# First layer of a four-layer decoder trunk: another order of loads, splits and transposes

## The chip, the core and the metric

The kernel runs on one core of a Trainium2 chip. The metric is the device time of one execution in microseconds (us), the median of several runs of the same program.

## The reference

Four residual layers follow each other, each `x = x + mixer(rms_norm(x, gain))`, on one sequence of 256 tokens with 1024 channels, all in float32. The mixers are of the kinds A, B, C, A. Only the beginning of the first one matters here:

```python
def rms_norm(x, g):
    y = x * lax.rsqrt(jnp.mean(x * x, axis=-1, keepdims=True) + EPS)
    return y * g

def mixer_a(h, w_in, v_gain, w_s, b_s, w_out):
    proj = h @ w_in                                   # (256, 1024) @ (1024, 6144)
    u = proj[..., :2048]
    v = rms_norm(proj[..., 2048:4096], v_gain)
    z = proj[..., 4096:]
    mixed = ...                                       # per chunk and group: tril(w_s) @ v + b_s
    return (u * mixed * jax.nn.silu(z)) @ w_out
```

## The kernel before

**Three products for one.** Every float32 operand is cut into a high part (a value of TensorE's fast float32 type, made by ACT) and a low part (what is left, made by DVE). A product of two such operands is three matmuls: high by high, high by low, low by high. In the list of engines PE is TensorE, ACT is ScalarE, DVE is VectorE, POOL is GpSimd, SP is SyncE.

**The weight stream.** All weights come through one stream of units `wr` of 128 x 1024 values (two K tiles of 128 rows by 512 columns). SP issues the loads (`load_units`, line 135) into four raw buffers, ACT writes the high part (`w0h`, `w1h`, ..., line 82), DVE the low part (`w0l`, ..., line 85), and a raw buffer comes free, so that SP loads the unit four further on, when DVE has written the low part. Seven pairs of split units are kept.

**The first projection (`proj_first`).** It makes the first 512 columns of `v` for both token tiles t = 0, 1 (two PSUM banks, `v_0` and `v_1`). K has eight tiles k = 0 to 7, in four pairs u. `turn(u)` is four TensorE transposes that bring the pair u of x, both token tiles, into one PSUM bank `hp`; `high(k)` is ACT's high part of h for one k, both token tiles (128x256, line 330, from `hp` to `hT`, with the gain `gT` as its scale); `low(k)` is DVE's low part (line 334); `w_high` and `w_low` split half a unit; `products(k)` is the six matmuls of one k (lines 77, 78, 79 in `mm3`). The row norms of x aren't needed here: their factor is put on later, and ACT takes the sums of squares (line 225) when the projection has been issued. Each engine works off its instructions in the order in which they stand in the code.

**After it** come the second `v` projection (units 4 and 5, then 6 and 7) and so on. Between them ACT squares the first projection's banks (line 494), DVE multiplies them with the gain (line 495), and both split the result (`v00h`, `v00l`) before they split unit 6.

**The loads at the start.** SP issues, in this order: x of token tile 0, columns 0 to 511 (256 KB); the first half of unit 0 (256 KB); x of token tile 1, columns 0 to 511; the second half of unit 0; unit 1 (512 KB); the other halves of x; units 2 and 3; a gain. ACT issues the 16 KB load of `gT`. TensorE does 13 transposes of an identity matrix (line 217) before there is data.

Of the kernel before, what the change touches and what calls it, by code (L numbers as in the profile page):

```python
# [10 lines left out]
F32 = mybir.dt.float32  # L11
F32R = mybir.dt.float32r
BF16 = mybir.dt.bfloat16
# [4 lines left out]
P = 128  # L18
D = 1024
S = 256  # L20
KT = D // P
HALF = 512
DEPTH = 4
# [25 lines left out]
def hybrid_trunk_kernel(ctx, tc, x, wts, norm_gainT, a_v_gain, a_wsT, a_bsT, b_gl, b_gv, c_scaleT,  # L49
                        masks, rope, rcnt, out):  # L50
    nc = tc.nc
    n_units = wts.shape[0]

    cp = ctx.enter_context(tc.tile_pool(name="cp", bufs=1))
# [4 lines left out]
    def pp(name):  # L59
        return ps.tile([P, HALF], F32, tag="pp", name=name, bufs=4)  # L60
# [7 lines left out]
    def tiny(n, name, tag="t"):  # L68
        return cp.tile([P, n], F32, tag=f"{tag}{n}", name=name, bufs=8)

    def pair(pool, shape, tag, name, bufs):
        return (pool.tile(shape, F32R, tag=tag + "h", name=name + "h", bufs=bufs),
                pool.tile(shape, F32R, tag=tag + "l", name=name + "l", bufs=bufs))

    def mm3(out_ap, lh, rh, start, stop):

        nc.tensor.matmul(out_ap, lh[0], rh[0], start=start, stop=False, skip_group_check=True)  # L77
        nc.tensor.matmul(out_ap, lh[0], rh[1], start=False, stop=False, skip_group_check=True)  # L78
        nc.tensor.matmul(out_ap, lh[1], rh[0], start=False, stop=stop, skip_group_check=True)  # L79

    def hi_of(hi, src):
        nc.scalar.activation(hi, src, AF.Copy)

    def lo_of(lo, src, hi):
        nc.vector.tensor_tensor(lo, src, hi.bitcast(F32), op=ALU.subtract)
# [16 lines left out]
    def tick():  # L102
        now[0] += 1
        if rms_due[0] and rms_due[0][0] <= now[0]:
            rms_due[0][1]()
            rms_due[0] = None
        for e in list(tasks):
            if e[0] <= now[0]:
                try:
                    e[0] = now[0] + next(e[1])  # L110
                except StopIteration:
                    tasks.remove(e)
# [12 lines left out]
    raws = []  # L125
    units = []
# [4 lines left out]
    def load_units(n):  # L131
        while loaded[0] < min(n, n_units):
            u = loaded[0]
            raw = wp.tile([P, 2, HALF], F32, tag="wr", name=f"wr{u}", bufs=RAW_BUFS)
            nc.sync.dma_start(raw, wts[u].rearrange("p (k n) -> p k n", n=HALF))
            raws.append(raw)
            loaded[0] += 1
# [3 lines left out]
    def split_hi(n):  # L141

        while split[0] < min(n, n_units):
            u = split[0]
            load_units(u + 1)
            hi, lo = pair(wp, [P, 2, HALF], "w", f"w{u}", W_BUFS)
            hi_of(hi, raws[u])
            units.append((hi, lo))
            split[0] += 1

    def split_units(n):

        split_hi(n)
        while lowered[0] < min(n, n_units):
            u = lowered[0]
            lo_of(units[u][1], raws[u], units[u][0])
            lowered[0] += 1
            load_units(u + 1 + RAW_BUFS)
# [14 lines left out]
            split_units(used[0] + ahead)  # L173


    xt = [cp.tile([P, D], F32, tag=f"x{t}", name=f"x{t}") for t in range(2)]

    def load_x(t, n):
        nc.sync.dma_start(xt[t][:, n * HALF:(n + 1) * HALF], x[t * P:(t + 1) * P, n * HALF:(n + 1) * HALF])


    raws.append(wp.tile([P, 2, HALF], F32, tag="wr", name="wr0", bufs=RAW_BUFS))
    loaded[0] += 1
    for t in range(2):
        load_x(t, 0)
        nc.sync.dma_start(raws[0][:, t], wts[0].rearrange("p (k n) -> p k n", n=HALF)[:, t])
    load_units(2)
    for t in range(2):
        load_x(t, 1)
    load_units(RAW_BUFS)  # L190
    kc_first = cp.tile([P, 3 * D], F32, tag="kc", name="kc0")
    nc.sync.dma_start(kc_first[:, :HALF], a_v_gain[0:1, :HALF].partition_broadcast(P))
    ident = cp.tile([P, P], F32, tag="ident", name="ident")
    make_identity(nc, ident)
    m05_row = cp.tile([P, 32], F32, tag="m05", name="m05")
    m05 = m05_row[:, :4]
    nc.gpsimd.memset(m05_row[:, :8], -0.5)
    r_rows = [m05_row[:, 8 * t + 8:8 * t + 9] for t in range(2)]
    junk = cp.tile([P, HALF + 32], BF16, tag="junk", name="junk")[:, :HALF]
    hT = cp.tile([P, 2 * KT * S + 16], F32R, tag="hT", name="hT")  # L200

    def gated(layer):

# [4 lines left out]
    def h_parts(layer):  # L208

        o = 16 if gated(layer) else 0  # L210
        return [hT[:, o + i * KT * S:o + (i + 1) * KT * S].rearrange("p (k s) -> p k s", s=S) for i in range(2)]
# [3 lines left out]
    warm = atp("warm")  # L215
    for _ in range(WARM):
        nc.tensor.transpose(warm[:, :P], ident, ident)
    gT = cp.tile([P, DEPTH, KT], F32, tag="gT", name="gT")
    nc.scalar.dma_start(gT, norm_gainT)

    nc.scalar.activation(junk[:, :4], m05, AF.Square)

# [1 line left out]
    def half_ss(t, n, ss):  # L224
        nc.scalar.activation(junk, xt[t][:, n * HALF:(n + 1) * HALF], AF.Square, scale=1.0 / 32.0,  # L225
                             accum_out=ss[:, n:n + 1])

    def norm_rms(layer, t, ss):
        ms = tiny(1, f"ms{layer}{t}")
        nc.vector.scalar_tensor_tensor(ms, ss[:, 0:1], EPS, ss[:, 1:2], op0=ALU.add, op1=ALU.add)  # L230
        r = r_rows[t] if gated(layer) else tiny(1, f"r{layer}{t}")
        r_tok[t] = r
        nc.gpsimd.tensor_tensor(r, ms, m05[:, 0:1], op=ALU.pow)  # L233
        return r
# [46 lines left out]
    def h_t(k, t):  # L281
        sl = slice(t * P, (t + 1) * P)
        return hcur[0][:, k, sl], hcur[1][:, k, sl]
# [29 lines left out]
    def proj_first(name):  # L313

        o = [pp(f"{name}_{t}") for t in range(2)]
        pts = {}
        hh, hl = h_parts(0)

        def turn(u):
            pts[u] = (trp if u == 3 else atp)(f"hp0{u}").rearrange("p (k t c) -> p k t c", t=2, c=P)  # L320
            for t in range(2):
                for k in range(2):
                    nc.tensor.transpose(pts[u][:, k, t], xt[t][:, (2 * u + k) * P:(2 * u + k + 1) * P], ident)

        def part(k):
            return pts[k // 2][:, k % 2].rearrange("p t c -> p (t c)"), gT[:, 0, k:k + 1]

        def high(k):
            pt, g = part(k)
            nc.scalar.activation(hh[:, k], pt, AF.Copy, scale=g)  # L330

        def low(k):
            pt, g = part(k)
            nc.vector.scalar_tensor_tensor(hl[:, k], pt, g, hh[:, k].bitcast(F32), op0=ALU.mult, op1=ALU.subtract)

        def w_pair(u):
            units.append(pair(wp, [P, 2, HALF], "w", f"w{u}", W_BUFS))
            split[0] += 1

        def w_high(u, kk):  # L340
            hi_of(units[u][0][:, kk], raws[u][:, kk])

        def w_low(u, kk):
            lo_of(units[u][1][:, kk], raws[u][:, kk], units[u][0][:, kk])
            if kk:
                lowered[0] += 1
                load_units(u + 1 + RAW_BUFS)

        def products(k):
            w = units[k // 2]  # L350
            for t in range(2):
                mm3(o[t], h_t(k, t), (w[0][:, k % 2], w[1][:, k % 2]), k == 0, k == KT - 1)

        turn(0)
        turn(1)
        w_pair(0)
        high(0)
        w_high(0, 0)
        high(1)
        w_high(0, 1)  # L360
        w_low(0, 0)
        low(0)
        low(1)
        w_low(0, 1)
        products(0)
        products(1)
        turn(2)
        high(2)
        high(3)
        w_pair(1)  # L370
        for kk in range(2):
            w_high(1, kk)
        low(2)
        low(3)
        for kk in range(2):
            w_low(1, kk)
        products(2)
        products(3)
        turn(3)
        for u in range(2, 4):  # L380
            high(2 * u)
            high(2 * u + 1)
            split_hi(u + 1)
            low(2 * u)
            low(2 * u + 1)
            split_units(u + 1)
            products(2 * u)
            products(2 * u + 1)
        used[0] += 4
        split_units(5)  # L390
        for t in range(2):
            ss = tiny(2, f"ss_{t}")
            for n in range(2):
                half_ss(t, n, ss)
            norm_rms(0, t, ss)
        split_units(6)
        for t in range(2):
            done.add(("h", 0, t))
        for _ in range(8):
            tick()  # L400
        return o
# [75 lines left out]
    def layer_a(layer, consts, pl, mid):  # L477
        hcur[:] = h_parts(layer)
        first = proj_first(f"v{layer}0") if layer == 0 else None
        kc, wsT, bsT = consts()  # L480

# [659 lines left out]
```

## Time and profile before

| | us |
|---|---|
| median of 3 runs (lowest, highest) | 840.42 (839.43, 840.59) |
| the profiled execution, its own time | 837.59 |
| its span, first to last instruction | 835.9 |
| PE busy in the span | 828.5 (99%), 4589 matmuls |
| DVE busy | 544.0 (65%) |
| ACT busy | 491.4 (59%) |
| POOL busy | 46.6 (6%) |

The granted TensorE clock is shown as full in all of the profile's 40 slices. The DMA engines moved 149.58 MB, a mean of 179 GB/s; in the first two slices (42 us) 271 and 283 GB/s. PE has 8 tenths in the first slice, 9 or more in all others up to the last one (8).

How to read it: PE bounds the kernel as a whole, and the other engines matter where PE waits for one of them. Where PE waits, and for what, stands in the view of waits; when that was, in the timeline.

### The profile page before, as it was taken

The page shows a single profiled execution, that of the slowest core. Times are in us where ns is not written, and L with a number is a line of the kernel's source. Part 1 is how long each engine was busy: PE and PEld are TensorE (multiplying, and loading weights), DVE is VectorE, ACT ScalarE, POOL GpSimd, SP SyncE. Part 2 cuts the span into 40 slices and gives each one's busy share as a digit, 9 for nine tenths or more (in the row PEclk, how much of TensorE's full clock was granted, in tenths as well). Part 3 has the DMA queues.
Part 4 walks back from the last instruction along what each step waited for, and adds up shares of the span by engine and source line. Part 5 has one row for each costly group of instructions (what it writes and reads, how often), then busy time and mean ns, then how long its engine had stood idle before and what let it go on. Part 6 is the DMA issues. An engine that isn't in the chain of part 4 may idle for free.

```text
span 835.9 us, 12347 instructions
## 1 busy us (share of the span) xinstructions
PE 828.5 (99%) x4589; PEld 717.5 (86%) x4589; DVE 544.0 (65%) x906; ACT 491.4 (59%) x913; POOL 46.6 (6%) x71
## 2 busy tenths in 40 slices
PE   8999999999999999999999999999999999999998
PEld 6788888888988888888888889999988888888886
DVE  4786656646757677577577576898754777556551
ACT  6775444436758688687687576455544666434340
POOL 0301000000000010010010021000000000000000
PEclk9999999999999999999999999999999999999999
DMA  7876565562745355345345168447564466454541
GB/s 271 283 247 223 177 201 176 177 198 83 253 166 182 107 158 191 107 160 187 108 161 186 58 224 280 160 140 256 198 223 155 131 241 208 159 184 161 176 151 51
DMA packets 41788, 149.58 MB, mean 179 GB/s; under 512 B 4896, under 2 KB 4912, under 8 KB 41600
## 3 DMA queue, kind: packets, MB, share of 16 engines
q1 hardware_dynamic: 40608, 144.98, 52.2%
q0 software_dynamic: 976, 3.79, 1.4%
q8 instruction: 36, 0.59, 0.3%
q14 instruction: 24, 0.20, 0.1%
q10 hardware_dynamic: 144, 0.02, 0.0%
HBM read 147.72 MB, written 1.05 MB: 178 GB/s over the span
## 4 chain that ended last, share of the span: by engine, by line
PE 96%; ACT 0%; DVE 0%; issue 0%
PE wo L77 6%; PE wo L79 6%; PE wo L78 6%; PE qk L77 5%; PE qk L79 5%; PE qk L78 5%; PE v L78 5%; PE v L79 5%; PE v L77 5%; PE z L79 3%; PE z L77 3%; PE z L78 3%; PE u L78 3%; PE u L77 3%; PE u L79 3%; PE cz L77 2%
## 5 line engine op out<-in xcount | busy, mean ns | idle before, releaser
L638 POOL TENSOR_TENSOR qr<-qm,m 128x8 f32<-128x8 f32 x12 | 19.7, 1638 | 227.9 <-DVE qm L637 227.9
L633 ACT ACTIVATE junk<-qk 128x128 bf16<-128x128 f32 x96 | 26.6, 277 | 7.3 <-PE qk L79 4.7
L554 DVE SCALAR_TENSOR_TENSOR sz<-u,m,sz 128x512 f32<-128x512 f32 x16 | 11.9, 747 | 27.9 <-PE u L79 27.9
L642 ACT ACTIVATE qn<-qk,qr 128x128 f32<-128x128 f32 x96 | 27.5, 381 | 3.4 <-POOL qr L638 3.4
L447 DVE TENSOR_TENSOR x<-wo,x 128x512 f32<-128x512 f32 x16 | 11.0, 690 | 20.1 <-PE wo L79 20.0
L251 ACT ACTIVATE hT<-hp,gT 128x128 fp32r<-128x128 f32 x48 | 13.0, 383 | 14.9 <-PE hp L247 14.9
L637 DVE TENSOR_SCALAR qm<-qs 128x8 f32<-128x8 f32 x12 | 2.1, 172 | 26.7 <-ACT junk L633 26.7
L256 DVE SCALAR_TENSOR_TENSOR hT<-hp,gT,hT 128x128 fp32r<-128x128 f32 x48 | 13.5, 345 | 8.8 <-ACT hT L251 8.8
L581 ACT ACTIVATE sz<-z,m 128x512 f32<-128x512 f32 x16 | 10.7, 686 | 13.9 <-PE z L79 13.9
L633 ACT ACTIVATION_READ_ACCUMULATOR junk<-qk 128x1 f32 x96 | 18.9, 197 | 0.0
L494 ACT ACTIVATE junk<-v,m 128x512 bf16<-128x512 f32 x16 | 11.0, 685 | 11.2 <-PE v L79 11.0
L495 DVE TENSOR_TENSOR vv<-v,kc 128x512 f32<-128x512 f32 x16 | 10.7, 687 | 8.4 <-ACT junk L494 8.0
L225 ACT ACTIVATE junk<-x 128x512 bf16<-128x512 f32 x16 | 10.2, 640 | 9.6 <-DVE x L447 9.4
L557 DVE SCALAR_TENSOR_TENSOR yy<-mx,bs,sz 128x256 f32<-128x256 f32 x32 | 14.0, 480 | 0.6
L663 PE MATMUL qt<-ident,qn 128*128 128x128 f32 x96 | 14.4, 272 | 0.0
L732 ACT ACTIVATE p<-p,rl 128x384 f32<-128x384 f32 (+1 forms) x16 | 11.5, 768 | 4.8 <-DVE rl L731 4.8
L655 DVE TENSOR_TENSOR rb<-qn,kcb 128x32 f32<-128x32 f32 x96 | 13.8, 185 | 0.0
L663 PEld LDWEIGHTS qt<-ident,qn 128*128 128x128 f32 x96 | 11.7, 140 | 2.3
L233 POOL TENSOR_TENSOR r<-ms,m 128x1 f32<-128x1 f32 x4 | 3.1, 784 | 175.3 <-DVE ms L230 175.3
L728 ACT ACTIVATE p<-p,nb 128x768 f32<-128x768 f32 x8 | 7.5, 937 | 7.6 <-DVE nb L727 7.6
L651 DVE TENSOR_TENSOR ra<-qn,kcb 128x64 f32<-128x64 f32 x48 | 10.6, 221 | 1.0 <-ACT qn L642 0.4
L473 POOL TENSOR_SCALAR_AFFINE_SELECT kc<-kc 128x128 f32<-128x128 f32 x16 | 9.1, 608 | 13.9 <-DMA kc<-in_a_wsT_dram 13.9
(2779 smaller groups left out, 3264.1 us busy)
## 6 DMA issues: line engine op xcount, KB each, us to landing
wr<-in_wts_dram SPq DMA_DIRECT2D x271, 512.0 KB, 3.8
x<-in_x_dram SPq DMA_DIRECT2D x4, 256.0 KB, 4.7
kc<-in_a_wsT_dram POOLq DMA_DIRECT2D x2, 512.0 KB, 8.1
kc<-in_a_v_gain_dram POOLq DMA_DIRECT2D x1, 1024.0 KB, 4.7
out_dram<-x SPq DMA_DIRECT2D x4, 256.0 KB, 2.0
kc<-in_a_v_gain_dram POOLq DMA_DIRECT2D x1, 768.0 KB, 7.4
kcb<-in_masks_dram POOLq DMA_DIRECT2D x1, 576.0 KB, 7.3
wr<-in_wts_dram SPq DMA_DIRECT2D x2, 256.0 KB, 4.1
```

Source lines behind the costliest of these rows:

```text
L77: nc.tensor.matmul(out_ap, lh[0], rh[0], start=start, stop=False, skip_group_check=True)
L78: nc.tensor.matmul(out_ap, lh[0], rh[1], start=False, stop=False, skip_group_check=True)
L79: nc.tensor.matmul(out_ap, lh[1], rh[0], start=False, stop=stop, skip_group_check=True)
L251: nc.scalar.activation(h_parts(layer)[0][:, k, t * P:(t + 1) * P], pt[:, k % 4], AF.Copy, scale=gT[:, layer, k:k + 1])
L256: nc.vector.scalar_tensor_tensor(hTl, pt[:, k % 4], gT[:, layer, k:k + 1], hTh.bitcast(F32), op0=ALU.mult, op1=ALU.subtract)
L554: nc.vector.scalar_tensor_tensor(us[t], up[t], r_tok[t][:, 0:1], us[t], op0=ALU.mult, op1=ALU.mult)
L557: nc.vector.scalar_tensor_tensor(y[:, sl], mxs[n][t][:, sl], bsT[:, 2 * n + gg:2 * n + gg + 1], us[t][:, sl], op0=ALU.add, op1=ALU.mult)
L633: nc.scalar.activation(junk[:, :HD], ov[t][:, h], AF.Square, accum_out=ssq[t][:, h:h + 1])
L638: nc.gpsimd.tensor_tensor(rqs, ms, m05_row[:, :8], op=ALU.pow)
L642: nc.scalar.activation(qn[t][:, h], ov[t][:, h], AF.Copy, scale=rq[t][:, h:h + 1])
L655: nc.vector.tensor_tensor(rb[:, hs, s0:s0 + 16], qn[t][:, hs, s1:s1 + 16], c, op=ALU.mult)
L663: nc.tensor.transpose(pts[t][:, h], qn[t][:, h], ident)
```

## The change

The first layer's beginning is written in another order.

- x becomes one tile `xx` of 128 x 2 x 1024, with both token tiles in it. Three loads by columns take the place of four by token tile: K tiles 0 and 1 of both token tiles (256 KB, in pieces of 1 KB), K tiles 2 and 3 (256 KB), K tiles 4 to 7 (512 KB).
- ACT issues the first half of unit 0, then `gT`. SP issues x for K tiles 0 and 1, the second half of unit 0, x for K tiles 2 and 3, unit 1, the rest of x, units 2 and 3.
- `products(k)` uses the low part of the weights last: for both token tiles high by high and low (of h) by high, then for both high by low (of w).
- `turn(1)` stands behind `products(0)` instead of ahead of it; `turn(2)` behind `products(2)`; `turn(3)` behind `products(3)`.
- ACT and DVE split in that order; the high parts of units 2 and 3 come next to each other, and ahead of `high(6)` and `high(7)`.

The number of matmuls, splits and bytes stays as it is. The loads:

```diff
-    xt = [cp.tile([P, D], F32, tag=f"x{t}", name=f"x{t}") for t in range(2)]
-
-    def load_x(t, n):
-        nc.sync.dma_start(xt[t][:, n * HALF:(n + 1) * HALF], x[t * P:(t + 1) * P, n * HALF:(n + 1) * HALF])
+    xx = cp.tile([P, 2, D], F32, tag="x", name="x")
+    xt = [xx[:, t] for t in range(2)]
+
+    def load_x(k0, k1):
+
+        nc.sync.dma_start(xx[:, :, k0 * P:k1 * P], x.rearrange("(t p) c -> p t c", p=P)[:, :, k0 * P:k1 * P])
...
-    for t in range(2):
-        load_x(t, 0)
-        nc.sync.dma_start(raws[0][:, t], wts[0].rearrange("p (k n) -> p k n", n=HALF)[:, t])
+    first_unit = wts[0].rearrange("p (k n) -> p k n", n=HALF)
+    gT = cp.tile([P, DEPTH, KT], F32, tag="gT", name="gT")
+    nc.scalar.dma_start(raws[0][:, 0], first_unit[:, 0])
+    nc.scalar.dma_start(gT, norm_gainT)
+    load_x(0, 2)
+    nc.sync.dma_start(raws[0][:, 1], first_unit[:, 1])
+    load_x(2, 4)
     load_units(2)
-    for t in range(2):
-        load_x(t, 1)
+    load_x(4, 8)
     load_units(RAW_BUFS)
...
-    gT = cp.tile([P, DEPTH, KT], F32, tag="gT", name="gT")
-    nc.scalar.dma_start(gT, norm_gainT)
```

The products, and the order as it is now:

```diff
         def products(k):
-            w = units[k // 2]
-            for t in range(2):
-                mm3(o[t], h_t(k, t), (w[0][:, k % 2], w[1][:, k % 2]), k == 0, k == KT - 1)
+
+            wh, wl = (a[:, k % 2] for a in units[k // 2])
+            for t in range(2):
+                for i, h in enumerate(h_t(k, t)):
+                    nc.tensor.matmul(o[t], h, wh, start=k == 0 and i == 0, stop=False, skip_group_check=True)
+            for t in range(2):
+                nc.tensor.matmul(o[t], h_t(k, t)[0], wl, start=False, stop=k == KT - 1, skip_group_check=True)
```

```python
        turn(0)
        w_pair(0)
        high(0)
        high(1)
        low(0)
        low(1)
        for kk in range(2):
            w_high(0, kk)
            w_low(0, kk)
        products(0)
        turn(1)
        high(2)
        w_pair(1)
        w_high(1, 0)
        high(3)
        w_high(1, 1)
        low(2)
        w_low(1, 0)
        low(3)
        w_low(1, 1)
        products(1)
        products(2)
        turn(2)
        high(4)
        high(5)
        split_hi(3)
        low(4)
        low(5)
        split_units(3)
        products(3)
        turn(3)
        products(4)
        split_hi(4)
        high(6)
        high(7)
        split_units(4)
        low(6)
        low(7)
        for k in range(5, KT):
            products(k)
```

On ACT the first data instructions stand like this before (`hp_112`, `hp_117`, `hp_146`, `hp_175` are the banks of the pairs 0 to 3; L330 is `high`, L82 a high part of weights, L225 a sum of squares):

```order
L330 ACTIVATE hT<-hp_112,gT 128x256
L82 ACTIVATE w0h<-wr_66 128x512
L330 ACTIVATE hT<-hp_112,gT 128x256
L82 ACTIVATE w0h<-wr_66 128x512
L330 ACTIVATE hT<-hp_117,gT 128x256 x2
L82 ACTIVATE w1h<-wr_71 128x512 x2
L330 ACTIVATE hT<-hp_146,gT 128x256 x2
L82 ACTIVATE w2h<-wr_75 128x1024
L330 ACTIVATE hT<-hp_175,gT 128x256 x2
L82 ACTIVATE w3h<-wr_77 128x1024
L82 ACTIVATE w4h<-wr_132 128x1024
L225 ACTIVATE junk,ss_230<-x_64 128x512 x2
```

and like this now (the banks are `hp_110`, `hp_133`, `hp_162`, `hp_183`; `high` is L334, the sum of squares L229):

```order
L188 DMA wr_65<-in_wts_dram 128x512
L189 DMA gT<-in_norm_gainT_dram 128x32
...
L334 ACTIVATE hT<-hp_110,gT 128x256 x2
L82 ACTIVATE w0h<-wr_65 128x512 x2
L334 ACTIVATE hT<-hp_133,gT 128x256
L82 ACTIVATE w1h<-wr_72 128x512
L334 ACTIVATE hT<-hp_133,gT 128x256
L82 ACTIVATE w1h<-wr_72 128x512
L334 ACTIVATE hT<-hp_162,gT 128x256 x2
L82 ACTIVATE w2h<-wr_75 128x1024
L82 ACTIVATE w3h<-wr_77 128x1024
L334 ACTIVATE hT<-hp_183,gT 128x256 x2
L82 ACTIVATE w4h<-wr_125 128x1024
L229 ACTIVATE junk,ss_228<-x 128x512 x2
```

Both high parts of pair 0 now stand ahead of the first weights, and the high part of unit 3 ahead of the high parts of pair 3.

On PE the piece from the first transposes of x to the third transposes stood like this (the six matmuls of k = 0, `v_0` ahead of `v_1`; those of k = 1 follow in the same order):

```order
L323 MATMUL hp_112<-ident,x_64 128x128 x2
L323 MATMUL hp_112<-ident,x_65 128x128 x2
L323 MATMUL hp_117<-ident,x_64 128x128 x2
L323 MATMUL hp_117<-ident,x_65 128x128 x2
L77 MATMUL v_0_110<-w0h,hT 128x512
L78 MATMUL v_0_110<-w0l,hT 128x512
L79 MATMUL v_0_110<-w0h,hT 128x512
L77 MATMUL v_1_111<-w0h,hT 128x512
L78 MATMUL v_1_111<-w0l,hT 128x512
L79 MATMUL v_1_111<-w0h,hT 128x512
```

and now, up to the first products of k = 2:

```order
L327 MATMUL hp_110<-ident,x 128x128 x4
L358 MATMUL v_0_108<-w0h,hT 128x512 x2
L358 MATMUL v_1_109<-w0h,hT 128x512 x2
L360 MATMUL v_0_108<-w0l,hT 128x512
L360 MATMUL v_1_109<-w0l,hT 128x512
L327 MATMUL hp_133<-ident,x 128x128 x4
L358 MATMUL v_0_108<-w0h,hT 128x512 x2
L358 MATMUL v_1_109<-w0h,hT 128x512 x2
L360 MATMUL v_0_108<-w0l,hT 128x512
L360 MATMUL v_1_109<-w0l,hT 128x512
L358 MATMUL v_0_108<-w1h,hT 128x512 x2
```

The transposes of pair 1 have moved behind the products of k = 0, and the low weight parts to the end of each k.

On DVE the pairs 0 and 1 of h and the units 0 and 1 are now taken like this (L338 is `low`, L85 a low part of weights):

```order
L338 SCALAR_TENSOR_TENSOR hT<-hp_110,gT,hT 128x256 x2
L85 TENSOR_TENSOR w0l<-wr_65,w0h 128x512 x2
L338 SCALAR_TENSOR_TENSOR hT<-hp_133,gT,hT 128x256
L85 TENSOR_TENSOR w1l<-wr_72,w1h 128x512
L338 SCALAR_TENSOR_TENSOR hT<-hp_133,gT,hT 128x256
L85 TENSOR_TENSOR w1l<-wr_72,w1h 128x512
```

Before, a half of `w0l` stood ahead of the low parts of pair 0 and the other behind them, and both low parts of pair 1 ahead of both halves of `w1l`. From the second projection on, all engines have the same instructions in the same order as before.

## Rows read from the trace of the kernel before

**Rows 1.** Waits of PE over the whole span: total us, times, longest.

```profile
...
PE v L77 <- ACT w0h L82: 0.6, 1, 0.6
PE hp L323 <- DMA x<-in_x_dram: 0.5, 1, 0.5
PE v L78 <- DVE w6l L85: 0.4, 1, 0.4
...
```

**Rows 2.** Windows: stretch, length, then busy us (count) of PE, PEld, DVE, ACT, POOL; granted clock; DMA share; GB/s.

```profile
1.43:4.47 3.04, 3.04 (x14) 3.04 (x15) 0.00 (x0) 1.30 (x2) 0.00 (x0) 1.00 0.76 234
...
26.45:835.90 809.45, 805.37 (x4487) 699.15 (x4487) 529.35 (x883) 473.05 (x879) 43.00 (x59) 1.00 0.53 176
```

**Rows 3.** Timeline, PE about the wait for unit 6: start us, us, engine, line.

```profile
26.45 0.50 PE L78 MATMUL v<-w6l,hT 128*128 128x512 f32 x1 [0.39 <-DVE w6l L85]
...
26.79 0.40 PE L79 MATMUL v<-w6h,hT 128*128 128x512 f32 x1
27.02 0.39 PE L77 MATMUL v<-w6h,hT 128*128 128x512 f32 x1
```

**Rows 4.** DMA issues, one short window each (0:1.0, 1.0:1.5, 1.5:2, 2:2.5): last figure us to landing.

```profile
x<-in_x_dram SPq DMA_DIRECT2D x1, 256.0 KB, 3.0
...
wr<-in_wts_dram SPq DMA_DIRECT2D x1, 256.0 KB, 3.5
...
x<-in_x_dram SPq DMA_DIRECT2D x1, 256.0 KB, 3.6
...
wr<-in_wts_dram SPq DMA_DIRECT2D x1, 256.0 KB, 4.8
```

**Rows 5.** Timeline of the start, the issues of those four loads on SP.

```profile
0.81 0.38 SPq L179 DMA_DIRECT2D x<-in_x_dram  x1
1.25 0.42 SPq L186 DMA_DIRECT2D wr<-in_wts_dram  x1
1.72 0.42 SPq L179 DMA_DIRECT2D x<-in_x_dram  x1
2.18 0.43 SPq L186 DMA_DIRECT2D wr<-in_wts_dram  x1
```

**Rows 6.** Timeline, from the first transposes of x to the first product.

```profile
5.37 1.13 PE L323 MATMUL hp<-ident,x 128*128 128x128 f32 x6 [0.48 <-DMA x<-in_x_dram]
...
6.10 0.47 ACT L330 ACTIVATE hT<-hp,gT 128x256 fp32r<-128x256 f32 x1 [3.37 <-PE hp L323]
6.47 0.62 ACT L82 ACTIVATE w0h<-wr 128x512 fp32r<-128x512 f32 x1
6.99 0.47 ACT L330 ACTIVATE hT<-hp,gT 128x256 fp32r<-128x256 f32 x1
...
7.14 0.49 PE L77 MATMUL v<-w0h,hT 128*128 128x512 f32 x1 [0.64 <-ACT w0h L82]
```

**Rows 7.** Timeline, the third and fourth transposes and what ACT and DVE make of them.

```profile
10.68 0.60 PE L323 MATMUL hp<-ident,x 128*128 128x128 f32 x4
...
11.03 0.48 PE L77 MATMUL v<-w1h,hT 128*128 128x512 f32 x1
...
11.32 0.84 ACT L330 ACTIVATE hT<-hp,gT 128x256 fp32r<-128x256 f32 x2 [1.57 <-PE hp L323]
...
12.04 1.06 ACT L82 ACTIVATE w2h<-wr 128x1024 fp32r<-128x1024 f32 x1
...
12.19 0.88 DVE L334 SCALAR_TENSOR_TENSOR hT<-hp,gT,hT 128x256 fp32r<-128x256 f32 x2 [1.00 <-ACT hT L330]
...
13.13 1.23 DVE L85 TENSOR_TENSOR w2l<-wr,w2h 128x1024 fp32r<-128x1024 f32 x1
...
16.19 1.06 ACT L82 ACTIVATE w4h<-wr 128x1024 fp32r<-128x1024 f32 x1
...
17.14 0.62 ACT L225 ACTIVATE junk<-x 128x512 bf16<-128x512 f32 x1
```

**Rows 8.** Timeline of PE alone in the window 6.2:6.5, transposes of x.

```profile
6.02 0.49 PE L323 MATMUL hp<-ident,x 128*128 128x128 f32 x3
```

More of the change, by code (lines that the diff above doesn't have):

```diff
@@ L194, in hybrid_trunk_kernel @@
     make_identity(nc, ident)
+    junk = cp.tile([P, HALF + 32], BF16, tag="junk", name="junk")[:, :HALF]
+    hT = cp.tile([P, 2 * KT * S + 16], F32R, tag="hT", name="hT")
     m05_row = cp.tile([P, 32], F32, tag="m05", name="m05")
@@ L198, in hybrid_trunk_kernel @@
     r_rows = [m05_row[:, 8 * t + 8:8 * t + 9] for t in range(2)]
-    junk = cp.tile([P, HALF + 32], BF16, tag="junk", name="junk")[:, :HALF]
-    hT = cp.tile([P, 2 * KT * S + 16], F32R, tag="hT", name="hT")
     def gated(layer):
@@ L349, in products @@
         def products(k):
-            w = units[k // 2]
+            wh, wl = (a[:, k % 2] for a in units[k // 2])
             for t in range(2):
-                mm3(o[t], h_t(k, t), (w[0][:, k % 2], w[1][:, k % 2]), k == 0, k == KT - 1)
+                for i, h in enumerate(h_t(k, t)):
+                    nc.tensor.matmul(o[t], h, wh, start=k == 0 and i == 0, stop=False, skip_group_check=True)
+            for t in range(2):
+                nc.tensor.matmul(o[t], h_t(k, t)[0], wl, start=False, stop=k == KT - 1, skip_group_check=True)
         turn(0)
-        turn(1)
         w_pair(0)
         high(0)
-        w_high(0, 0)
         high(1)
-        w_high(0, 1)
-        w_low(0, 0)
         low(0)
         low(1)
-        w_low(0, 1)
+        for kk in range(2):
+            w_high(0, kk)
+            w_low(0, kk)
         products(0)
+        turn(1)
+        high(2)
+        w_pair(1)
+        w_high(1, 0)
+        high(3)
+        w_high(1, 1)
+        low(2)
+        w_low(1, 0)
+        low(3)
+        w_low(1, 1)
         products(1)
+        products(2)
         turn(2)
[L368 to L377, printed above, removed]
+        high(4)
[4 more added lines that the diff above has]
+        split_units(3)
         products(3)
         turn(3)
[L380 to L388, printed above, removed]
+        products(4)
[7 more added lines that the diff above has]
+            products(k)
         used[0] += 4
```

## Prediction

> **What bounds the kernel now.** I read the page first: PE is busy for 99% of the span, so the kernel is as long as PE's work plus PE's waits. Then the waits of PE alone: apart from the start of its warm-up there are four, and the three largest are 0.6, 0.5 and 0.4 us [rows 1]; all of them lie in the first 27 us. Then the windows: from 26.45 us on PE is busy for 805.37 us and waits for nothing until only the last additions and stores are left [rows 2]. So what follows 26.45 us is a fixed block, whose instructions the change leaves as they are, and the question has one number in it: when does PE get past its last wait, that for the low part of unit 6, which ended at 26.45 [rows 3]?
>
> That wait ends a chain, which I follow back in the timeline. After its last weights for the first projection ACT starts the sums of squares at 17.14 [rows 7]; the sums, unit 5's high part, the squares of the first projection, its two high parts, unit 6's high part and DVE's low part of it follow without room and end at 26.45, 9.31 us later. I keep these 9.31 us as one term, since no instruction in them changes. Ahead of 17.14 ACT is driven by the transposes of x.
>
> **Where the change acts.** All of it lies before that point. I write T0, T1, T2 for the starts of the transposes of pairs 0, 1 and 2.
>
> *T0, the first x.* Before, x of token tile 0 was issued at 0.81 and landed 3.0 us later, at 3.8; the first weights at 1.25, landing at 4.75; x of token tile 1 at 1.72, landing at 5.3; the second half of unit 0 at 2.18, landing at 7.0 [rows 4, 5]. PE started the second half of its turn of pair 0 at 5.37 [rows 6]. Now one load of 256 KB, issued first, suffices. At best it lands like the first load did, and PE takes it up when the 13 warm-up transposes let it, 4.3 (they and a 14th end at 4.47 [rows 2]). At worst it is as late as the third was, 5.3, if its smaller pieces and ACT's load beside it cost that much. The first two loads, 512 KB together, were there at 4.75, and now two of that size start at the same moment; I take **T0 = 4.6**, a little better than both together, since x is first on its own queue. Here the Trainium skill speaks against the change: its page "DMA: Bandwidth & Descriptors", section "Issuing engines are not separate DMA queues", says that transfers from several engines run on the same 16 DMA engines and interleave, so that only issue time is saved. By that rule the first x and the first weights would both be there at about 4.75 and the sum below would be 0.15 us more; no row of before shows two large loads from two queues.
>
> *From T0 to the first product.* From 5.37, with two transposes of pair 0 to go, ACT's first `high` followed at 6.10, 0.73 later [rows 6]. Now four have to be done, and transposes were still slow by then: 14 of them took 3.04 us (0.22 each) [rows 2], while three later ones took 0.49 in all [rows 8]. Two more at 0.22 make 1.17. If they are fast, it is 0.64, as for pair 2 (10.68 to 11.32 [rows 7]), plus 0.1 for a start from rest. I take 1.17. Then come two `high` in place of one ahead of the first weights: 2 x 0.37 (6.10 to 6.47), then 0.67 from the weights' split to the product (6.47 to 7.14) [rows 6]. First product: 4.6 + 1.17 + 0.74 + 0.67 = 7.18, where it was 7.14. What the earlier x gives, the order on ACT and the slow transposes take back. The second half of unit 0 is one load earlier in SP's queue and needed at about 7.0, so I count no wait for it; `gT`, now behind 256 KB on ACT's queue, is needed at 5.8 and is tiny.
>
> *T1.* Products run at 0.23, the one after a wait at 0.34 (26.45, 26.79, 27.02 [rows 3]). Six take 0.34 + 5 x 0.23 = 1.48; with the low weights last none of them waits for DVE. T1 = 7.18 + 1.48 = 8.66.
>
> *T2.* The turn costs PE 0.35 (10.68 to 11.03 [rows 7]), the six products of k = 1 1.46, so PE is at k = 2 at T1 + 1.81. Its high part is there, but the next product needs `low(2)`. In the trace DVE's first `low` of a pair begins only when ACT has finished **both** `high` of the pair: 12.19, where the two ran from 11.32 to 12.16 [rows 7]. Both read one PSUM bank, and DVE waited for ACT's last reading of it. Now a weight split stands between the two `high`: `high(2)` at T1 + 0.64, `w_high` 0.37 later, `high(3)` 0.52 after that (6.47 to 6.99 [rows 6]), done 0.47 later at T1 + 2.00; `low(2)` takes 0.45 (half of 0.88) and with the signals PE goes on at T1 + 2.53. That is a **new wait of 0.49 us**. Five products from there (0.34 + 4 x 0.23) put T2 at T1 + 3.78 = 12.44.
>
> *From T2 to the end of the chain.* Now ACT has, without a break: `high(4)`, `high(5)` from T2 + 0.64; unit 2 0.72 later (11.32 to 12.04); unit 3 0.95 later (16.19 to 17.14, a full unit); `high(6)`, `high(7)` another 0.95; unit 4 0.72; the sums of squares 0.95 [rows 7]. Sum: T2 + 4.93. With the 9.31 of above PE passes its last wait at T2 + 14.24 = **26.68**, 0.23 later than before. PE itself would be there slightly sooner: it waits for unit 2's high part until T2 + 2.47 (0.64 + 0.72 + 1.06 and a signal), for its low part until 3.73 (1.23 more), and the 45 products from there to the second of unit 6 take it to T2 + 14.1. So the chain through ACT decides, and smaller shifts on PE cost nothing; if that cover were gone, each would count in full.
>
> Sum: the profiled execution took 837.59 and would take 837.8. The median of the runs is 840.42, 2.8 us above it, and gets the same 0.2: **840.6**. About 0.2% (1.7 us) is what a measurement of this kernel can tell from no change.
>
> Ends of the unknown terms: T0 = 4.3 with fast transposes gives T2 = 11.7 and 0.5 us less; T0 = 5.3 with slow ones 0.9 more. So this case spans 839.9 to 841.4.
>
> **The rivals.**
> 1. *The gain comes whole.* x at 4.3, fast transposes, and `low(2)` starts without `high(3)`: no wait of 0.49, and no 0.11 for going on after it. T2 is 11.1, the last wait ends 1.1 us sooner, 839.3. For it: the waits of [rows 1] are real. Against it: the row at 12.19, and that even this is 0.14%.
> 2. *Slower: TensorE's clock.* Its place is the start. The granted clock reads 1.00 there, which is 2.4 GHz, yet transposes run at half pace at first [rows 2, 8], as at 1.2 GHz; it had doubled by 6.02, after the warm-up and the first five transposes of x. Now PE has four transposes instead of eight between the warm-up and the first product, and rests from about 5.7 to 7.2. If the pace is still half up to the middle of k = 1, ten products at 0.46 cost 2.3 us; 0.6 of it falls into the wait for `low(2)`, so 1.7 and the 0.2 from above: 842.3. From nine such products on it decides the sign. Against it: the warm-up is the same. In the Trainium skill the page "TensorE: Matmul & The Clock Gate", section "What's actually happening", has the rule behind it: throttled is the default state, and activity releases the throttle.
> 3. *x is later than 5.3*, by its 1 KB pieces and the shared engines; each tenth counts in full, so x at 5.8 gives 842.0. Then the change does nothing of what it says. Rows of before have no such load.
>
> **How the numbers follow.** The forecast has 0.70, rival 1 0.10, rival 2 0.14, rival 3 0.06. Faster by over 0.2% (below 838.7) is out of reach of every sum; I leave half of rival 1 for what the runs scatter, 0.05. Slower by over 0.2% (above 842.1): 0.11 of rival 2 and 0.02 of rival 3, 0.13. The rest, 0.82, is within 0.2%. The range goes from 839.1, below rival 1, to 842.3, where rival 2 begins.
>
> **What would show it.** First transposes of x near 4.6; first product near 7.2; a wait of PE for DVE's `low(2)` of about 0.5 us near 10.5; a wait of ACT's making for unit 2's high part; turn 2 near 12.4; PE past unit 6's low part near 26.7, with nothing after it. I am wrong if that last number is below 25.5 or above 28, if products of k = 0 are 0.4 apart, or if PE waits anywhere later.

## The result, and where the time went

| | us |
|---|---|
| changed kernel, median of 20 runs (lowest, highest) | 841.73 (839.43, 842.46) |
| kernel before, median of 20 runs beside them | 839.56 (837.46, 840.66) |
| ratio, with its 95% interval | 1.0025 (1.0017 to 1.0033) |
| profiled execution of the changed kernel, its own time and span | 839.43, 837.7 |
| the same of the kernel before | 837.59, 835.9 |

The kernel became slower by 0.25%, some 2.2 us, where 0.2 us were forecast. The profiled executions differ by nearly as much: 1.8 us of span. I take that difference apart with the views that carried the prediction. The waits of PE in the changed kernel (total us, times, longest):

```profile
PE v L358 <- ACT w0h L82: 1.4, 1, 1.4
PE warm L223 <- POOL m L205: 1.4, 1, 1.4
PE v L358 <- DVE hT L338: 0.3, 1, 0.3
```

The waits for x and for unit 6's low part [rows 1] are gone from this list, the predicted one for DVE's `low(2)` is in it, and nothing later. The timeline of PE from the first transposes of x on, and its three rows about unit 6 (start us, us, engine, line; in brackets the idle time before and what ended it):

```profile
4.52 0.66 PE L327 MATMUL hp<-ident,x 128*128 128x128 f32 x4
6.62 1.20 PE L358 MATMUL v<-w0h,hT 128*128 128x512 f32 x4 [1.45 <-ACT w0h L82]
...
8.18 0.60 PE L327 MATMUL hp<-ident,x 128*128 128x128 f32 x4
...
10.75 0.96 PE L358 MATMUL v<-w1h,hT 128*128 128x512 f32 x3 [0.33 <-DVE hT L338]
...
12.01 0.60 PE L327 MATMUL hp<-ident,x 128*128 128x128 f32 x4
...
25.87 0.39 PE L77 MATMUL v<-w6h,hT 128*128 128x512 f32 x1
26.27 0.50 PE L78 MATMUL v<-w6l,hT 128*128 128x512 f32 x1
26.60 0.40 PE L79 MATMUL v<-w6h,hT 128*128 128x512 f32 x1
```

PE is past the point that the forecast rests on at 26.27, where it was 26.45 [rows 3]: the start is 0.18 us **better**. (A short wait is still there: 25.87 to 26.27 is 0.40, and 0.23 is the pace.) So the loss lies behind it. The window from there to the end, in the columns of [rows 2]:

```profile
26.27:837.70 811.43, 807.36 (x4487) 700.55 (x4487) 529.52 (x883) 472.91 (x879) 42.84 (x59) 1.00 0.53 176
```

The same 4487 matmuls keep PE busy for 807.36 us in place of 805.37 [rows 2], 1.99 us more. What is not busy is 4.07 us, where it was 4.08. So: 0.18 us gained at the start, 1.99 lost in work that the change doesn't touch, no new wait; together the 1.8.

To find the place I compared, unit by unit of the weight stream, when PE starts on it. The changed kernel is 0.2 us ahead at unit 7, level by unit 107, 0.4 behind at unit 160, 1.7 at unit 172 and 1.8 at the end. Most of it falls on units 158 to 171, in the third layer, where `hT` moves in pieces of 128x256. Two windows there, from the first matmul of unit 158 to that of unit 176, of the changed kernel

```profile
509.10:559.90 50.80, 50.80 (x434) 50.80 (x433) 39.92 (x58) 23.98 (x31) 0.50 (x4) 1.00 0.55 186
```

and of the kernel before:

```profile
508.90:558.20 49.30, 49.30 (x435) 49.30 (x435) 39.06 (x56) 23.67 (x30) 0.50 (x4) 1.00 0.56 191
```

PE is busy all the time in both, at a granted clock of 1.00, and takes 1.5 us longer for the same matmuls. What sets it off shows in the timeline of PE. Kernel before:

```profile
507.13 0.60 PE L890 MATMUL czt<-ident,czs 128*128 128x128 f32 x4
...
507.69 0.28 PE L78 MATMUL cz<-hT,w157h 128*128 128x256 f32 x1
...
508.94 0.28 PE L77 MATMUL cz<-hT,w158h 128*128 128x256 f32 x1
...
510.19 0.28 PE L79 MATMUL cz<-hT,w158l 128*128 128x256 f32 x1
```

Changed kernel:

```profile
507.16 0.28 PE L79 MATMUL cz<-hT,w157l 128*128 128x256 f32 x1
507.28 0.60 PE L903 MATMUL czt<-ident,czs 128*128 128x128 f32 x4
...
507.84 0.28 PE L78 MATMUL cz<-hT,w157h 128*128 128x256 f32 x1
...
509.14 0.28 PE L77 MATMUL cz<-hT,w158h 128*128 128x256 f32 x1
...
510.43 0.28 PE L79 MATMUL cz<-hT,w158l 128*128 128x256 f32 x1
```

Eleven matmuls go from 508.94 to 510.19 before (0.1136 each) and from 509.14 to 510.43 now (0.1173 each). Ahead of the four transposes `czt` the pace is 0.113 in both. Behind them the changed kernel keeps the slower one through unit 171, some 340 matmuls. (Units 172 and 173 are other matmuls, of a tile `cg`, and nearly as slow in the kernel before: 2.85 us a unit, now 2.88.) The length of the records tells the two paces apart at a glance. Unit 164 before (count, then least, median and greatest ns, first and last start):

```profile
L77 PE MATMUL cx<-hT,w164h x8: 276/277/277, 525.3 to 527.6; 128*128 128x256 f32 x8
```

and in the changed kernel:

```profile
L77 PE MATMUL cx<-hT,w164h x8: 281/281/281, 526.1 to 528.6; 128*128 128x256 f32 x8
```

The instructions and their order are the same there. What isn't the same is where the tiles lie. The change creates `gT` ahead of `kc` and the identity `ident` (the first diff above shows the line), and `junk` and `hT` ahead of a small row `m05`. In the compiled program `ident` moves from byte 36992 of each partition to 37120, `kc` from 24704 to 24832, `gT` and `m05` change ends; `hT` and `junk` stay where they were. Three of the seven buffers for low weight parts change places too. `ident` is an operand of every transpose, `czt` among them.

### The profile page after: what moved, and what is told of

The parts are those of the page before. It is cut to its first block, busy times and chain, and to the rows that moved or that the text cites. A ratio compares the mean times of both kernels' runs of the same rounds, so it can differ in the third digit from the quotient of the medians.

```text
span 837.7 us, 12345 instructions
## 1 busy us (share of the span) xinstructions
PE 830.2 (99%) x4589; PEld 718.2 (86%) x4589; DVE 544.1 (65%) x906; ACT 491.2 (59%) x913; POOL 46.4 (6%) x71
## 4 chain that ended last, share of the span: by engine, by line
PE 98%; ACT 1%; DMA 0%; DVE 0%; issue 0%
PE wo L77 6%; PE wo L79 6%; PE wo L78 6%; PE qk L77 5%; PE qk L79 5%; PE qk L78 5%; PE v L77 5%; PE v L78 5%; PE v L79 5%; PE z L77 4%; PE z L78 3%; PE z L79 3%; PE u L77 3%; PE u L78 3%; PE u L79 3%; PE cx L77 2%
## 5 line engine op out<-in xcount | busy, mean ns | idle before, releaser
L594 ACT ACTIVATE sz<-z,m 128x512 f32<-128x512 f32 x16 | 10.7, 686 | 14.0 <-PE z L79 13.9
L229 ACT ACTIVATE junk<-x 128x512 bf16<-128x512 f32 x16 | 10.3, 641 | 9.6 <-DVE x L460 9.4
L508 DVE TENSOR_TENSOR vv<-v,kc 128x512 f32<-128x512 f32 x16 | 10.7, 687 | 7.8 <-ACT junk L507 7.4
L922 ACT ACTIVATE xc<-cx 128x512 f32<-128x512 f32 x8 | 4.7, 596 | 9.0 <-PE cx L79 8.7
```

## The experiments

Two theories: the loss comes from the **addresses** that the change moves by the way, or from the **order** of the first layer, by something it leaves behind. A third matter came up with the first runs: the median lies 2.3 us above the profiled execution for the changed kernel, 2.0 to 2.8 for the one before.

Each kernel was timed beside the kernel before on one chip, and its profile read. The ratio is taken over the single runs and isn't the quotient of two medians of this table, since the kernel before has other runs, and another median (839.15 to 839.83), beside each group. "Record" is the median length in ns of the matmuls of unit 164. "Growth" is how much further behind the first profile of the kernel before a kernel is at unit 259 than at unit 7, in us; it leaves out what happens at the start.

| kernel | order | byte of `ident` | median us (runs) | ratio (95%) | record | growth |
|---|---|---|---|---|---|---|
| r_before | before | 36992 | 839.93 (11) | 1.0002 (0.9992 to 1.0011) | 276 | 0.0 |
| r_after | changed | 37120 | 842.20 (11) | 1.0026 (1.0017 to 1.0036) | 281 | 2.0 |
| after, the profile above | changed | 37120 | 841.73 (20) | 1.0025 (1.0017 to 1.0033) | 281 | 2.0 |
| e1 | changed | 36992 | 839.63 (12) | 0.9995 (0.9986 to 1.0005) | 276 | 0.0 |
| e2 | before | 37120 | 840.94 (12) | 1.0014 (1.0004 to 1.0025) | 281 | 2.0 |
| e3 | changed | 36992 | 839.43 (11) | 0.9999 (0.9989 to 1.0008) | 276 | 0.0 |
| e4 | changed | 37120 | 841.72 (10) | 1.0025 (1.0016 to 1.0035) | 281 | 2.0 |
| e5 | changed | 37120 | 842.20 (9) | 1.0031 (1.0021 to 1.0041) | 281 | 2.0 |
| e11 | changed | 38080 | 841.63 (12) | 1.0020 (1.0010 to 1.0031) | 281 | 1.7 |
| e8 | changed | 37120, a copy for `czt` | 838.69 (11) | 0.9997 (0.9987 to 1.0007) | 276 | 0.4 |
| e7 | changed, PE filled | 36992 | 838.28 (11) | 0.9994 (0.9986 to 1.0003) | 276 | 0.0 |
| e9 | changed, PE filled, `high(3)` first | 36992 | 837.91 (11) | 0.9980 (0.9971 to 0.9989) | 276 | 0.0 |
| e10 | before, PE filled | 36992 | 837.88 (11) | 0.9980 (0.9971 to 0.9988) | 276 | 0.0 |

**The two kernels again**, without an edit. The kernel before:

> The kernel before once more. Theory A: again the fast pace through units 158 to 171, and a ratio of 1.000 +- 0.001. Theory B: the pace through these units can be the slow one here too, with a profiled time about 1.5 us longer.

The changed kernel:

> The changed kernel once more, for its scatter. In its first profile PE passes its wait for unit 6's low part 0.18 us sooner than before, and the 1.8 us of its span are lost where layer C multiplies units 157 to 172, at 0.117 us for a product instead of 0.113. Theory A (something fixed in the program, such as the addresses that the change moved, sets that pace): the same stretch is slow again, and the ratio is 1.0025 +- 0.0008. Theory B (the pace is set anew in each execution): the slow stretch lies elsewhere or is missing in this profile, and the total goes with it. Theory S (the start is slower): the wait for unit 6's low part ends later than 26.45.

The difference came again, 0.0026. Both profiles happened to catch an execution whose first products run at half pace; I come back to that below. The slow stretch lies in the same place again, so it belongs to the program and not to the single execution.

**e1: the changed order with the addresses of before.** The tiles are created in an order that gives each its old address; nothing else is touched.

```diff
+    kc_first = cp.tile([P, 3 * D], F32, tag="kc", name="kc0")
+    ident = cp.tile([P, P], F32, tag="ident", name="ident")
+    m05_row = cp.tile([P, 32], F32, tag="m05", name="m05")
+    junk = cp.tile([P, HALF + 32], BF16, tag="junk", name="junk")[:, :HALF]
+    hT = cp.tile([P, 2 * KT * S + 16], F32R, tag="hT", name="hT")
     gT = cp.tile([P, DEPTH, KT], F32, tag="gT", name="gT")
```

> The changed kernel with the tiles gT, m05, ident and kc at the addresses that they had before (the low weight buffers stay as the change has them). Theory A in the form that the small tiles' addresses set the pace: units 158 to 171 run at 0.113, ratio 1.000 or a little less. The order or the weight buffers set it: still 0.117 there, ratio 1.0025. Theory S: no difference to the changed kernel, 1.0025, and the loss shows ahead of 27 us.

**e2: the order of before with the addresses of the change**, the same edit the other way round:

```diff
+    gT = cp.tile([P, DEPTH, KT], F32, tag="gT", name="gT")
+    kc_first = cp.tile([P, 3 * D], F32, tag="kc", name="kc0")
+    ident = cp.tile([P, P], F32, tag="ident", name="ident")
+    junk = cp.tile([P, HALF + 32], BF16, tag="junk", name="junk")[:, :HALF]
+    hT = cp.tile([P, 2 * KT * S + 16], F32R, tag="hT", name="hT")
+    m05_row = cp.tile([P, 32], F32, tag="m05", name="m05")
```

> The kernel before with gT, m05, ident and kc at the addresses of the changed kernel, order of work untouched. Theory A (small tiles' addresses): slow pace in units 158 to 171, ratio 1.0025. Otherwise 1.000.

The loss goes with the addresses. With the old ones the changed order is not slower (0.9995), with the new ones the old order is (1.0014, less than expected, but with the whole growth of 2.0 us). The buffers of low weight parts are out of it: e1 has them where the change puts them and is fast, e2 has them in their old places and is slow. What the order itself is worth is too small to be told here.

**e3, e4, e5: which tile.** Edits of e1's list, from its order (`kc`, `ident`, `m05`, `junk`, `hT`, `gT`). In e3 only `gT` and `m05` lie elsewhere than before, in e4 `m05`, `kc` and `ident`, with the last two 128 bytes up; in e5 `ident` is 128 bytes up and `kc` isn't (`gT` lies between them, `m05` where the change has it).

```diff
-e1: kc, ident, m05, junk, hT, gT
+e3: kc, ident, gT, junk, hT, m05
+e4: m05, kc, ident, junk, hT, gT
+e5: kc, gT, ident, junk, hT, m05
```

> The changed kernel with kc and ident at their addresses of before; gT and m05 stay away from theirs (m05 where the change has it, gT where m05 was). Theory I (ident or kc sets the pace of units 158 to 171): 0.113 us a product there, ratio to before 1.000 +- 0.001. Theory M (m05 or gT sets it): 0.117, 1.0025.

> The changed kernel with gT where it was before and m05 just ahead of kc, so that kc and ident stay 128 bytes further on, as the change has them. Theory I: slow pace, 1.0025. Theory M: fast, 1.000.

> The changed kernel with gT between kc and ident: kc at its old address, ident 128 bytes further on as the change has it, m05 as the change has it. If ident's place sets the pace: slow, 1.0025. If kc's does: fast, 1.000.

It is `ident`. With it in the old place, where `gT` and `m05` lie makes no difference; with it 128 bytes up, e5 has the whole loss though `kc` stays. Unit 164 in e5:

```profile
L77 PE MATMUL cx<-hT,w164h x8: 281/282/282, 528.8 to 531.3; 128*128 128x256 f32 x8
```

**e8: the changed kernel with a second identity for `czt` alone**, eight transposes in two groups of four. All other transposes keep the moved one. The copy lies at byte 57472, whose distance to the old place is a multiple of 4096.

```diff
+            spare = cp.tile([P, 2, HALF], F32, tag="xs", name="ident2", bufs=1)
+            ident2 = spare[:, 0, 320:320 + P]
+            nc.vector.tensor_scalar(ident2, ident, 1.0, None, op0=ALU.mult)
...
-                        nc.tensor.transpose(st[:, c0:c0 + P], sz[t][:, (2 * i + k) * P:(2 * i + k + 1) * P], ident)
+                        nc.tensor.transpose(st[:, c0:c0 + P], sz[t][:, (2 * i + k) * P:(2 * i + k + 1) * P], ident2)
```

> The changed kernel, ident where the change has it, but the transposes of the gate in layer C (the ones just ahead of the slow stretch) read a copy of the identity that DVE makes at another address, whose last 12 bits are those of ident's old address. If the operand of these transposes sets the pace that the following products keep: fast (0.113 us) through units 158 to 171, ratio 1.000 to 1.0005. If ident acts in another way (as a neighbour in memory, say): slow, 1.0025.

The pace after the transposes is the fast one, in unit 164 of e8:

```profile
L77 PE MATMUL cx<-hT,w164h x8: 276/276/276, 526.2 to 528.6; 128*128 128x256 f32 x8
```

So the place of the identity that these few transposes read decides the pace that the many matmuls **behind** them keep. The rest of the growth fits that too: e8 loses 0.2 us between units 7 and 143 and 0.2 behind them. The other kernels with the moved identity lose as much between those two (0.2 to 0.3, e11 0.1), those with the old one nothing, and e8's other transposes use the moved one.

**e11: a third address**, 1088 bytes above the old one (`junk` and `m05` move below and above it):

```diff
+    junk = cp.tile([P, HALF + 32], BF16, tag="junk", name="junk")[:, :HALF]
     ident = cp.tile([P, P], F32, tag="ident", name="ident")
     m05_row = cp.tile([P, 32], F32, tag="m05", name="m05")
-    junk = cp.tile([P, HALF + 32], BF16, tag="junk", name="junk")[:, :HALF]
```

> The changed kernel's order of work, with the addresses of e1 but the identity 1088 bytes above the old place (38080 in place of 36992; the changed kernel has it 128 above, at 37120), by exchanging it with the scratch row next to it; hT, kc and gT stay as in the kernel before. Theory A, that only the place 128 bytes up is bad (its distance to other operands within some short period): the matmuls of unit 164 have records of 276 ns, ratio 0.999 to 1.0005 against the kernel before. Theory B, that the old place is the good one and any other low bits of the address are bad: 281 ns, ratio 1.0015 to 1.0035. A third value of the record, neither 276 nor 281, would say that the pace has more than two values.

281 ns and 1.0020: slow too. For the matmuls behind `czt` the old low part of the address is the only fast one of the three that were tried.

It isn't a good address as such, though. In the second layer four groups of transposes `qt` stand each ahead of 24 such matmuls, and there the traces show the same two paces, in another pattern. At unit 88 the **old** place is the slow one. Kernel before:

```profile
265.59 0.28 PE L78 MATMUL v2p<-w88l,hT 128*128 128x256 f32 x1
...
266.77 0.28 PE L79 MATMUL v2p<-w88h,hT 128*128 128x256 f32 x1
```

Changed kernel:

```profile
265.57 0.28 PE L78 MATMUL v2p<-w88l,hT 128*128 128x256 f32 x1
...
266.71 0.28 PE L79 MATMUL v2p<-w88h,hT 128*128 128x256 f32 x1
```

Ten matmuls take 1.18 us before and 1.14 now. At units 106 and 142 it is the other way round, at unit 124 both are slow; at these four units the runs that share a place of `ident` agree. Behind the first of the two groups `czt` (505.47 in the changed kernel) the pace is the fast one with the moved identity as well. So the kernel before has slow stretches of its own, and moving the identity deals them out anew. The whole is slower because the second group `czt` stands ahead of some 340 matmuls and each of these `qt` ahead of 24.

**The first products at half pace.** In r_before, the kernel before itself, the timeline of PE reads:

```profile
5.86 1.54 PE L323 MATMUL hp<-ident,x 128*128 128x128 f32 x6 [0.97 <-DMA x<-in_x_dram]
7.63 0.79 PE L77 MATMUL v<-w0h,hT 128*128 128x512 f32 x1 [0.23 <-ACT w0h L82]
...
12.36 0.63 PE L78 MATMUL v<-w0l,hT 128*128 128x512 f32 x1
12.79 0.62 PE L79 MATMUL v<-w0h,hT 128*128 128x512 f32 x1
13.22 0.63 PE L323 MATMUL hp<-ident,x 128*128 128x128 f32 x4
13.61 0.48 PE L77 MATMUL v<-w1h,hT 128*128 128x512 f32 x1
```

Its products are 0.43 apart up to 13.2, not 0.23, and it is 2.5 us behind at unit 7. The window of these products, in the columns of [rows 2]:

```profile
7.63:13.22 5.59, 5.59 (x13) 3.96 (x14) 4.05 (x8) 2.71 (x6) 0.00 (x0) 1.00 1.02 393
```

The granted clock stands at 1.00, the level of 2.4 GHz, while the pace is about that of 1.2. The 1.00 is not a reading: in the trace the records of the granted clock begin at 13.27, at full, which is where the pace doubles. Ahead of that there is no record, and the views count time without one as full. So by pace and records together these products ran at the lower level. The warm-up does so in every profile, with 0.21 us or more from one transpose to the next, and the first record comes behind it: at 5.96 in the profile of the kernel before that the prediction read, at 4.39 in that of the changed kernel.

In r_after it is as in r_before: first product 7.51, half pace up to 12.8, first record at 12.94, and 2.5 us behind at unit 7. Over all 14 profiles the start follows this moment. Where the first record begins between 4.4 and 6.0 a kernel is 0.2 us ahead to 0.6 behind at unit 7; between 10.3 and 10.7 (e1, e3, e4) 1.8 to 2.1 behind; between 12.9 and 13.3 (r_before, r_after, e5, e11) 2.5. So both kernels have it alike, and since the first profiles of both were of executions with an early clock, it is what separates those from the medians. PE rests between the warm-up and the first product; three kernels fill these rests with transposes of the identity.

**e7: e1 with PE filled**, behind `turn(0)`:

```diff
         turn(0)
+        for _ in range(6):
+            nc.tensor.transpose(warm[:, :P], ident, ident)
```

> The changed kernel with the old addresses (as e1), and six more transposes of the identity behind the first transposes of x, where PE rests for 1.4 us until the first weights are split. Most executions of both kernels take until 11 to 13 us for TensorE's pace to double, and lose some 2.5 us so. Theory C (PE's rest is what keeps the pace low): the pace doubles sooner in most executions, the median falls by 1 to 2 us against e1, to a ratio of about 0.998. Otherwise: as e1, 0.9995.

Its products are at full pace in the profile, with the first record of the clock at 5.42. Of its 11 runs 2 lie over 1 us above its fastest; of the changed kernel 15 of 20 do, of the one before 16 of 20. Its median is 1.35 us below that of e1, but the kernel before was 0.68 us faster beside it too, and the ratio of 0.998 that was expected was missed: 0.9994 can't be told from 1, nor from e1's 0.9995.

**e9: e7 with `high(3)` ahead of unit 1's high parts**, for the wait for `low(2)`:

```diff
         high(2)
+        high(3)
         w_pair(1)
         w_high(1, 0)
-        high(3)
         w_high(1, 1)
```

> As the filled start with the old addresses (e7), and ACT makes the high part of K tile 3 ahead of the first half of unit 1. By the prediction's step for K tile 2, DVE's low part of it starts 0.5 us sooner after its high part, PE's wait of 0.3 us for it goes, and PE waits 0.2 to 0.3 us for the weights' high part instead: turn 2 is 0.2 to 0.3 us sooner, and so is the end. Median 0.2 us below e7, a ratio of about 0.999; not to be told apart by the times, so the waits decide.

The wait is gone. All waits of PE in e9:

```profile
PE warm L222 <- POOL m L204: 1.4, 1, 1.4
PE v L357 <- ACT w0h L82: 0.8, 1, 0.8
PE hp L326 <- DMA x<-in_x_dram: 0.4, 1, 0.4
```

As expected, the turn of pair 2 is 0.28 us sooner than in e7 (12.34, 12.62), and PE is past unit 6's low part as much sooner (26.60, 26.88). That is no sooner than in the kernel before, though. None of its 11 runs lies over 1 us above the fastest.

**e10: the kernel before with PE filled**, three transposes while it waits for x of token tile 1, three behind `turn(1)`, and nothing of the change:

```diff
+        def fill(n):
+            for _ in range(n):
+                nc.tensor.transpose(warm[:, :P], ident, ident)
...
+                if u == 0 and t == 0:
+                    fill(3)
...
         turn(1)
+        fill(3)
```

> The kernel before with three transposes of the identity while PE waits for x of token tile 1 and three more while it waits for the first weights. Theory C (rest keeps the pace low): most executions double their pace before the first product, and the median falls by about 2 us, to 837.5 to 838 and a ratio of 0.998. If it does nothing, the ratio is 1.000 and the executions go on to spread over 3 us.

e9 and e10 beat both kernels, by 0.2% against the one before, and are equal (837.91 and 837.88). So with the identity in its old place and PE kept busy, the order of the change adds nothing that these runs can tell. One edit of six transposes has the whole gain.

## Why the prediction was right and wrong

**Right, by its steps.** The profiled execution of the changed kernel against the working:

| step | forecast | measured |
|---|---|---|
| T0, first transposes of x | 4.6 | 4.52 |
| first product | 7.18 | 6.62 |
| T1 | 8.66 | 8.18 |
| wait for `low(2)` | 0.49 | 0.33 |
| T2 | 12.44 | 12.01 |
| sums of squares on ACT, T2 + 4.93 | 17.37 | 16.93 (T2 + 4.92) |
| past unit 6's low part | 26.68 | 26.27 |

The two loads: the first x landed 3.7 us after its issue at 0.81, at 4.5, and ACT's first weights at 4.0:

```profile
x<-in_x_dram SPq DMA_DIRECT2D x2, 256.0 KB, 4.0
...
wr<-in_wts_dram ACTq DMA_DIRECT2D x1, 256.0 KB, 3.2
```

(The window is 0 to 3 us; the 4.0 is the median of x's two 256 KB loads, 3.7 and 4.3.) Alone at the head of the queue x had taken 3.0 [rows 4]. The Trainium skill says on its page "DMA: Bandwidth & Descriptors", section "Issuing engines are not separate DMA queues", that transfers started by different engines share the DMA engines; the trace agrees, since by 3.0 us the queues had moved 0.20 MB in both profiles, nearly all of it SP's before (0.19) and ACT's now (0.17). 512 KB were there by 4.5 where it was 4.75. Whether the smaller pieces of x cost something as well was not tried, and the two loads took 4.1 and 3.8 in r_after.

The one term at the start that was mis-sized is the time from T0 to the first `high`, 1.17 by slow transposes. It took 0.70 in this execution, where the clock was granted in full at 4.39, just ahead of T0, and 1.16 in r_after (4.95 to 6.11), where it came at 12.94. The wait for `low(2)` is 0.33 for the reason given: DVE starts at 10.21, after ACT's second `high` of the pair (9.71 to 10.18), and e9, which puts the two `high` together, has no such wait. It is a wait of the program: the compiled `low(2)` asks for the count of the semaphore that the second `high` raises. The 9.31 us behind the start of the sums, kept as one term, took 9.34; they aren't quite "without room", since ACT waits 0.37 in them for DVE, before and after alike.

**Wrong, by one step: "what follows 26.45 us is a fixed block, whose instructions the change leaves as they are".** The instructions are the same, and yet it took 1.99 us more of PE, without any wait. The step took equal instructions for equal time, and the diff for an order of work only. It also moves tiles, and which of two paces a matmul of 128x256 keeps hangs on where an operand of the transposes ahead of it lies (e1, e2, e5, e8). In the profiled execution the sum is 0.2 forecast, less 0.4 by which the start came out better than worked out, plus 2.0 from this step: the 1.8 measured. In the medians (2.2) the start's gain doesn't show, since r_before and r_after are both 2.5 us behind at unit 7. The prediction's own test, that it is wrong if PE waits anywhere later, couldn't have found this, since nothing waits. Comparing the busy time of a stretch with equal instruction counts does.

**What was luck.** The median, 841.73, lies in the range from 839.1 to 842.3, but for a reason that isn't in the prediction: the upper part of the range was there for a late x and for a slow clock in the changed kernel alone, and neither made the difference. By the ratio the kernel is slower by over 0.2%, an outcome that was given 0.13. That the start came out 0.4 us better than worked out is luck too: it hangs on when the clock was granted in that execution.

**The rivals.** The first (the whole gain) didn't come: the wait for unit 0's high part grew from 0.64 [rows 6] to 1.45, and ate most of what the earlier x gave. The third (x later than 5.3) didn't come; by its own terms, 0.5 us above the case of 5.3, it gives 841.9 and not 842.0. The second is half right: first products at half pace do occur and cost some 2.5 us, but in both kernels, so that its 842.3 lies near the measured median is chance. It took the 1.00 of the window [rows 2] for a reading of the clock; the first record of that trace begins at 5.96, just ahead of the first fast transposes at 6.02 [rows 8]. In the Trainium skill the page "TensorE: Matmul & The Clock Gate", section "What's actually happening", calls the throttled state the default, which activity releases; e9 and e10 fit that, for with PE kept busy the runs over 1 us above the fastest all but vanish (0 and 1 of 11).

**Still open.** Why an operand's address decides the pace of the matmuls behind it, and what else does, since one place of `ident` is fast behind one group of transposes and slow behind another: three places and one copy were tried, and `hT` wasn't moved. What decides when the clock is granted in full in a given execution without the filling: in the profiles the first x is later in some that get it late (r_after 4.95 with a rest of 0.49 ahead, against 4.52), but e8 waited 0.4 for it as well and has its first record at 5.84. What the order of the change is worth by itself is within the interval of e1.

## What to carry to other kernels

An edit that creates a tile earlier can move the tiles behind it, and so change more than its diff shows: when parts of a kernel that weren't touched get slower without a new wait, compare PE's busy time over the same count of matmuls, then the addresses. Pin the addresses (create tiles in the old order) before judging a reordering, or the two effects are read as one. Don't read the old place as the good one: it is slow behind other transposes of the same kernel. Where the median lies well above the profiled execution, look at the pace of the first matmuls, and see whether the trace has a record of the clock there at all, since a 1.00 can stand for none. Filling PE's rests between the warm-up and the first data was worth 0.2% here (e10), some 1.7 us, more than the 1.1 us that the reordering could have brought by the first rival.

## What the runs showed of the hardware

- The 128x256 matmuls of these kernels have two paces. Moving the identity by 128 or by 1088 bytes within its partition slowed those behind the second group `czt` from 0.1136 to 0.1173 us each (record 276 to 281 ns). The slower pace lasted some 340 matmuls, through unit 171, and the kernel loses 1.7 to 2.0 us to it and to shorter stretches like it. At unit 88 moving it by 128 bytes made them faster (0.118 to 0.114).
- In an execution of either kernel PE can run at half pace up to 10 or 13 us, and by the times most do: 0.43 in place of 0.23 us per 128x512 matmul. In the trace the records of the clock begin, at full, where this ends (13.27 in r_before); a 1.00 that a view shows ahead of that stands for no record. Six more transposes in PE's rests brought the runs that lie over 1 us above the fastest from 16 of 20 down to 1 of 11 (e10).
- The order of two `high` on ACT was worth a wait of 0.33 us on PE, since the program lets DVE's first `low` of a pair start only behind the second `high` (10.18, and 10.21). Whether the two engines could read one PSUM bank together was not tried.
